# Making the low parts of split weights by accumulating transfers instead of VectorE subtractions

## The chip, the cores and the metric

One core of a Trainium2 chip. The metric is the device time of one execution in microseconds (us); lower is better.

## The reference, cut to what matters

Two layers over 1024 latent and 256 context tokens (NT = 1280 columns), everything in float32.

```python
xa, ga, ub, gb = split(h @ w_in)                     # layer 0, 3072 output channels
u = dwconv_centred(xa, conv_w, conv_b)               # 8 heads of 128 channels
r, i = sigmoid(u @ wr[d] + br), sigmoid(u @ wi[d] + bi)   # d = 0, 1: two directions
a = exp(-8 * r * softplus(-lam)); b = sqrt(-expm1(2 * log_a)) * (i * u)
ya = scan(a, b, forward) + scan(a, b, backward)      # RG-LRU recurrence
yb = s5(ub); yb = yb * sigmoid(gelu(yb) @ glu_w + glu_b)
out = concat([ya * silu(ga), yb * silu(gb)]) @ w_out # 12 blocks of 128 channels
# layer 1: latent attention, 8 heads; not touched by the change
```

## The kernel before, in words

A float32 product is computed as three matmuls of `fp32r` parts: each operand is split into a rounded high part `hi` and a low part `lo = x - hi`, and `mm3` adds hi·hi, hi·lo and lo·hi. The low part of a weight is needed first by the third matmul of a group, that of an activation by the second. Before the change every split is one ScalarE copy (`hi`, L182, L964, L1196) and one VectorE subtraction (`lo`, L184, L968, L1198).

Layer 0 runs in this order: a start; the recurrences of 8 heads; the output projection `out0`. The recurrences are written out by hand: `TURNS` is a list of words for turn 0 and 1, for turns 2 to 6 and for turn 7, and each engine executes its instructions in just that order. A word is a letter, arguments and an age (`-` is the head of the next turn). The words that matter here:

- `W`: splits a loaded weight tile (`wraw`, one buffer; `wh` and `wl`, two each) and then, in `load`, issues the next tile's load on SP's queue. `P`: one block of columns (256, 512 or 512) of the current tile's product; three make a tile. There are 18 tiles of gates and heads, 4 of `glu`, 16 of `out`; all but the first, which the start splits, go through `W`.
- `U`, `V`: load and split the gate weights of one direction of a head. `G`: a gate's product and its sigmoid.
- `C`: a tap of the convolution on VectorE. `I`, `O`: high and low part of a head's convolved input.
- `E`: one step of `s5_weights` (turns 0 and 1); its last step in each of 8 passes multiplies four groups of 32 output rows into one PSUM bank (L526, L529).
- `k a s r d o`: a batch of the S5 scan; `r` clears two columns by memsets on GpSimd (L1023, L1024), and VectorE's copy L1025 waits for them. `l` loads for it.
- `N`, `Y`: the scans of a head; its results go to DRAM by GpSimd's queue, the second one adding onto the first (`accum_op`, L953).
- In turn 7, `F` loads a head's result and gate, `S` multiplies them and splits the product (12 such pairs with `X` and `T` fill `self.mix` and `y`), `K` multiplies the S5 branch. Their tiles come from one pool of 11 slots (`big`); a load on SP's queue waits there until a slot is free, and all loads behind it wait too.

In `out0` the 16 `out` tiles run six `P` to a pair of tiles, with `W` after the first and the fourth.

Of the kernel before, what the change touches and what calls it, by code (L numbers as in the profile page):

```python
# [9 lines left out]
F32 = mybir.dt.float32  # L10
F32R = mybir.dt.float32r
AF = mybir.ActivationFunctionType
ALU = mybir.AluOpType
# [12 lines left out]
C1 = 6.28125  # L26
C2 = float(np.float32(np.round((2 * math.pi - C1) * 2 ** 21) / 2 ** 21))
# [5 lines left out]
def shape_constants():  # L33
# [18 lines left out]
    for a in (row, col):  # L52
# [13 lines left out]
     "E0 E0 E0 G000 E0 E0 E0 E0 V1- E0 E0 E0 V0- W0 A00 H00 P0 E0 E0 E0 E0 E0 E0 C0- P0 B00 "  # L66
     "W0 Y1 E0 A10 E0 Q00 E0 P0 E0 E0 E0 E0 E0 E0 C1- C2- I- P0 E0 O-").split(),
    ("D01 H11 M11 k21 U1- Q11 a21 G000 l00 N01 P0 G100 s21 B11 r21 U0- d21 D11 N11 W0 P0 o21 l10 a00 "
     "k00 s00 P0 r00 d00 C1- W0 Y1 P0 G110 o00 k10 G010 a10 C0- s10 M00 V0- V1- C2- A10 r10 A00 H00 I- Q00 "
     "d10 P0 O- l20 P0 B00 o10").split(),  # L70
# [62 lines left out]
class Kernel:  # L133
# [62 lines left out]

    def weight_parts(self, raw):
        return self.split(raw, self.wp, "w", 2, list(raw.shape))

    def raw_uk(self, h):  # L200
        return self.raw_weights(self.t["w_uk"][h], 2)
# [257 lines left out]
    def s5_weights(self, Pre, Pim, bb, ccp):  # L459

        nc, sp = self.nc, self.sp
        tt, stt = nc.vector.tensor_tensor, nc.vector.scalar_tensor_tensor
        scr = self.s5scr = self.dram.tile([16, 128, 4, 2, 128], F32, name="s5scr")

        seq = self.s5seq = self.dram.tile([32, 16, 256], F32, name="s5seq")
        vx = lambda *shape: self.tl(sp, [128, *shape], "vx", 4)
        b4 = lambda a, m: a.unsqueeze(2).to_broadcast([128, 4, m, 16])
        p4 = lambda a: a.unsqueeze(3).to_broadcast([128, 4, a.shape[2], 16])
        for Q in range(8):
            gs = slice(4 * Q, 4 * Q + 4)  # L470
            if Q % 4 == 0:

                Kt = self.tl(sp, [128, 4, 144], "s5K", 1)
                pads = []
                for k in range(2):
                    p = self.tl(sp, [128, 16, 32], "pad", 2)
                    nc.gpsimd.memset(p, 0.0)
                    hg = slice(4 * Q, 4 * Q + 16)
                    nc.vector.tensor_copy(p[0:64, :, 0:16], bb[0:64, k, hg])
                    nc.vector.tensor_copy(p[64:128, :, 16:32], bb[64:128, k, hg])  # L480
                    pads.append(p)

            Vs = []
            for k in range(2):
                V, x = vx(4, 8, 16), vx(4, 8, 16)
                pr, pi = p4(Pre[:, gs, 0:8]), p4(Pim[:, gs, 0:8])
                tt(x, pi, b4(bb[:, 1 - k, gs], 8), ALU.mult)
                tt(V, pr, b4(bb[:, k, gs], 8), ALU.mult)
                Vs.append((V, x))
                yield  # L490
            for k, (V, x) in enumerate(Vs):
                tt(V, V, x, ALU.subtract if k == 0 else ALU.add)
                pt = self.bank([128, 4, 128], "s5", 2)
                for g in range(4):
                    nc.tensor.transpose(pt[:, g], V[:, g].rearrange("p j h -> p (j h)"), self.ident)
                st = self.tl(sp, [128, 4, 128], "st", 2)
                nc.scalar.copy(st, pt)
                self.stores.append((scr[2 * Q:2 * Q + 2, :, k].rearrange("b p g n -> p b g n"),
                                    st.rearrange("p (b g) n -> p b g n", b=2)))
                yield  # L500

            Cs = []
            for k in range(2):
                C, x = vx(4, 9, 16), vx(4, 9, 16)
                pr, pi = p4(Pre[:, gs, 8:17]), p4(Pim[:, gs, 8:17])
                tt(x, pi, b4(ccp[:, 1 - k, gs], 9), ALU.mult)
                tt(C, pr, b4(ccp[:, k, gs], 9), ALU.mult)
                Cs.append((C, x))
                yield
            for k, (C, x) in enumerate(Cs):  # L510
                if k == 0:
                    tt(C, C, x, ALU.subtract)
                else:
                    stt(C, C, -1.0, x, ALU.mult, ALU.subtract)
                for b in range(2):
                    self.stores.append((scr[2 * Q + b, :, 2 + k],
                                        C[:, 2 * b:2 * b + 2, 1:9].rearrange("p g m h -> p g (m h)")))
                yield
            Cs = [C for C, _ in Cs]
            pk = self.bank([128, 144], "s5", 2)  # L520
            for g4 in range(4):
                g = 4 * Q + g4
                o = pk[32 * g4:32 * g4 + 32]
                for k in range(2):
                    C = Cs[k][:, g4].rearrange("p m h -> p (m h)")
                    nc.tensor.matmul(o[:, 16:144], pads[k][:, g % 16], C[:, 16:144], start=(k == 0), stop=(k == 1))  # L526
                for k in range(2):
                    both = bb[:, k, g:g + 2].rearrange("p g h -> p (g h)")
                    nc.tensor.matmul(o[:, 0:16], both, Cs[k][:, g4, 0], start=(k == 0), stop=(k == 1))  # L529
            nc.scalar.copy(Kt[:, Q % 4], pk)  # L530
            stt(Kt[:, Q % 4, 0:16], self.dmask, self.s5d[:, Q:Q + 1], Kt[:, Q % 4, 0:16], ALU.mult, ALU.add)
            if Q % 4 == 3:
                dst = seq[4 * Q - 12:4 * Q + 4].rearrange("(q g) h n -> g h q n", g=4)
                for g4 in range(4):
                    a = 32 * g4
                    self.stores.append((dst[g4, :, :, 128:256], Kt[a:a + 16, :, 0:128]))
                    self.stores.append((dst[g4, :, :, 0:128], Kt[a + 16:a + 32, :, 16:144]))
            yield
# [349 lines left out]
    def recurrences(self, steps):  # L888
# [3 lines left out]
        nc = self.nc  # L892
# [4 lines left out]
        class Head:  # L897
# [6 lines left out]
                nc.sync.dma_start(x.raw[d], self.t["gate_w"][x.h, :, 2 * d:2 * d + 2])  # L904

            def V(x, d):
                x.gw[d] = self.split(x.raw.pop(d), self.gp, "gw", 2, [128, 2, 128])

            def G(x, d, q):

# [53 lines left out]
                nc.scalar.copy(x.hi, self.us[x.h][0])  # L964

            def O(x):
                lo = self.big([128, NT], F32R, name="lo")
                nc.vector.tensor_sub(lo, self.us[x.h][0], x.hi.bitcast(F32))  # L968
                self.us[x.h] += x.hi, lo

        class Batch:
# [31 lines left out]
            def s(x):  # L1003

                x.t2 = self.s5t([128, 2, 2, NCH], "t2")
                x.G = self.s5t([128, 2, 2, EXT], "G")
                S = x.G[:, :, :, 0:NCH]
                for g in range(2):
                    tt(x.t2[:, :, g], x.ph[:, 1:3, g], x.p[g][:, ::-1], ALU.mult)
                    tt(S[:, :, g], x.p[g], x.ph[:, 0, g].unsqueeze(1).to_broadcast([128, 2, NCH]), ALU.mult)  # L1010
                tt(S, S, x.t2, ALU.add)
                nc.vector.tensor_copy(x.G[:, :, :, NCH:EXT], x.G[:, :, :, 0:32])
# [45 lines left out]
        class Tiles:  # L1058
            n, b, n_raw = 0, 0, 1
            raws, ws, ps = [], [self.first], {}  # L1060

            def load(x):
                if x.n_raw < len(tiles):
                    kind, i, _ = tiles[x.n_raw]
                    src, k = {"glu": (t["glu_w"], 4), "out": (t["w_out"], 6)}.get(kind, (t["w_in"], 8))
                    src = src[i // 2, :, 6 * (i % 2):6 * (i % 2) + 6] if kind == "out" else src[i]
                    x.raws.append(self.raw_weights(src, k))
                    x.n_raw += 1

            def W(x):  # L1070
                if x.raws:
                    x.ws.append(self.weight_parts(x.raws.pop(0)))
                    x.load()

            def P(x):
# [4 lines left out]
                kind, i, out = tiles[x.n]  # L1080
                b = x.b
                s, z = BLK[b]
                w = x.ws[0]
                src = {"glu": lambda: x.y, "out": lambda: self.mix[6 * (i % 2):6 * (i % 2) + 6]}.get(kind, lambda: self.n0)()
                if kind != "out" or i % 2 == 0:
                    x.ps[b] = self.bank([128, z], "g" if kind == "out" and i % 4 else "mm", 3)
                p, n = x.ps[b], len(src)
# [5 lines left out]
                elif kind == "gate":  # L1093
                    o = self.row((128, z))
# [11 lines left out]
                    x.ws.pop(0)  # L1106


            yg, y, g, gb, m, ga = {}, [None] * 4, {}, {}, {}, {}

            def Z(x, i):
                self.store()
# [19 lines left out]
                nc.sync.dma_start(x.ga[h], self.gadr[h])  # L1132

            def S(x, h):
                m, g = x.m.pop(h), x.ga.pop(h)
                nc.vector.tensor_mul(m, m, g)
                self.mix[h] = self.split_big(m, alloc=self.far)

            def J(x, i):
                x.gb[i] = self.big(name="gb")  # L1140
# [694 lines left out]
```

## Time and profile before

| | |
|---|---|
| time of three executions, median (lowest to highest) | 1578.91 us (1574.0 to 1582.47) |
| the profiled execution, its own time | 1579.79 us |
| its span, first to last instruction | 1577.7 us |
| mean granted TensorE clock | 0.981 |
| busy share of the span: TensorE, VectorE, ScalarE, GpSimd | 94%, 72%, 52%, 3% |

PE is TensorE's matmuls, PEld its weight loads, DVE is VectorE, ACT ScalarE, POOL GpSimd, SP the queue that issues most loads. L184 is line 184 of the kernel before. Clocks are shares of full speed. Busy shares are means over stages: turns 0 and 1 run from about 140 to 274 us, turns 2 to 6 to about 522, turn 7 to 655, `out0` to 820.

### The profile page before, as it was taken

The page shows a single profiled execution, that of the slowest core. Times are in us where ns is not written, and L with a number is a line of the kernel's source. Part 1 is how long each engine was busy: PE and PEld are TensorE (multiplying, and loading weights), DVE is VectorE, ACT ScalarE, POOL GpSimd, SP SyncE. Part 2 cuts the span into 40 slices and gives each one's busy share as a digit, 9 for nine tenths or more (in the row PEclk, how much of TensorE's full clock was granted, in tenths as well). Part 3 has the DMA queues.
Part 4 walks back from the last instruction along what each step waited for, and adds up shares of the span by engine and source line. Part 5 has one row for each costly group of instructions (what it writes and reads, how often), then busy time and mean ns, then how long its engine had stood idle before and what let it go on. Part 6 is the DMA issues. An engine that isn't in the chain of part 4 may idle for free.

```text
span 1577.7 us, 22599 instructions
## 1 busy us (share of the span) xinstructions
PE 1486.9 (94%) x8690; PEld 1277.5 (81%) x8690; DVE 1138.1 (72%) x1856; ACT 828.3 (52%) x1424; POOL 46.8 (3%) x107
## 2 busy tenths in 40 slices
PE   7899898988988996999999999999999999999997
PEld 4677777877777785878788999888999999999887
DVE  7678788999999888422255625558888888889655
ACT  7457766766866684110143414446555565566532
POOL 0001000000000000000000000010000000000000
PEclk9999999999999998999999999999999999999999
DMA  9355444644655555645351231451120120122353
GB/s 353 135 182 182 163 145 143 180 143 132 193 142 157 167 194 201 230 167 180 134 217 54 81 93 34 152 188 44 31 66 26 64 58 18 40 94 87 105 175 114
DMA packets 96154, 207.76 MB, mean 132 GB/s; under 512 B 9904, under 2 KB 42416, under 8 KB 96048
## 3 DMA queue, kind: packets, MB, share of 16 engines
q1 hardware_dynamic: 86528, 166.65, 32.3%
q0 software_dynamic: 9520, 39.69, 7.6%
q8 instruction: 68, 1.11, 0.3%
q14 instruction: 38, 0.31, 0.1%
HBM read 143.03 MB, written 63.28 MB: 131 GB/s over the span
## 4 chain that ended last, share of the span: by engine, by line
PE 35%; issue 26%; DVE 11%; DMA 2%; ACT 1%; POOL 1%; SPq 0%; DVEq 0%; POOLq 0%; ACTq 0%
PE pv L1580 7%; PE pt L1567 4%; PE S L209 2%; PE S L211 2%; PE S L210 2%; PE S L1519 2%; PE S L1518 2%; PE S L1517 2%; PE S L1516 2%; PE S L1515 2%; DVE H L1020 1%; PE mm L211 1%; PE mm L209 1%; PE mm L210 1%; PE pt L210 1%
## 5 line engine op out<-in xcount | busy, mean ns | idle before, releaser
L182 ACT CAST w_hi<-wraw 128x1024 fp32r<-128x1024 f32 (+3 forms) x73 | 63.3, 867 | 182.6 <-PE mm L210 130.5
L209 PE MATMUL mm<-n0hi,w_hi 128*128 128x512 f32 (+1 forms) x432 | 156.8, 363 | 0.0
L210 PE MATMUL mm<-n0lo,w_hi 128*128 128x512 f32 (+1 forms) x432 | 154.7, 358 | 0.0
L211 PE MATMUL mm<-n0hi,w_lo 128*128 128x512 f32 (+1 forms) x432 | 153.9, 356 | 0.0
L1571 ACT CAST ph<-pt 128x512 fp32r<-128x512 f32 x160 | 91.0, 590 | 83.2 <-PE pt L1567 82.9
L1574 DVE TENSOR_TENSOR pl<-pt,ph 128x512 fp32r<-128x512 f32 x160 | 109.5, 686 | 19.7 <-ACT ph L1571 17.7
L209 PE MATMUL mm<-hi,w_hi 128*128 128x512 f32 (+1 forms) x264 | 100.4, 380 | 11.5 <-ACT w_hi L182 9.5
L209 PE MATMUL mm<-n1hi,w_hi 128*128 128x342 f32 (+2 forms) x336 | 109.6, 329 | 1.7 <-DVE pr L1323 1.7
L210 PE MATMUL mm<-n1lo,w_hi 128*128 128x342 f32 (+2 forms) x336 | 110.2, 328 | 0.0
L211 PE MATMUL mm<-n1hi,w_lo 128*128 128x342 f32 (+2 forms) x336 | 110.1, 328 | 0.0
L1580 PE MATMUL pv<-ph,v 128*128 128x256 f32 x640 | 107.4, 298 | 0.0
L211 PE MATMUL mm<-hi,w_lo 128*128 128x512 f32 (+1 forms) x264 | 98.9, 378 | 5.1 <-DVE w_lo L184 5.1
L210 PE MATMUL mm<-lo,w_hi 128*128 128x512 f32 (+1 forms) x264 | 98.9, 375 | 0.1
L209 PEld LDWEIGHTS mm<-n0hi,w_hi 128*128 128x128 f32 x432 | 82.0, 190 | 12.8
L211 PEld LDWEIGHTS mm<-n0hi,w_lo 128*128 128x128 f32 x432 | 81.7, 189 | 12.7
L210 PEld LDWEIGHTS mm<-n0lo,w_hi 128*128 128x128 f32 x432 | 81.9, 190 | 12.1
L1567 PE MATMUL pt<-c_ident,P 128*128 128x128 f32 x640 | 90.9, 272 | 0.6 <-DVE kl L1497 0.6
L184 DVE TENSOR_TENSOR w_lo<-wraw,w_hi 128x1024 fp32r<-128x1024 f32 (+3 forms) x73 | 72.3, 991 | 25.9 <-ACT w_hi L182 24.9
L1552 ACT ACTIVATE P<-S,sm 128x512 f32<-128x512 f32 x128 | 86.8, 689 | 0.0
L1580 PEld LDWEIGHTS pv<-ph,v 128*128 128x128 f32 x640 | 84.3, 190 | 0.2
L1567 PEld LDWEIGHTS pt<-c_ident,P 128*128 128x128 f32 x640 | 75.7, 140 | 10.4 <-DVE kl L1497 0.8
L1544 DVE TENSOR_REDUCE sm<-S 128x1 f32<-128x512 f32 x128 | 82.0, 680 | 0.8 <-PE S L1519 0.8
(424 smaller groups left out, 4013.9 us busy)
## 6 DMA issues: line engine op xcount, KB each, us to landing
mw<-in_mod_w SPq DMA_DIRECT2D x48, 512.0 KB
wraw<-in_w_in SPq DMA_DIRECT2D x24, 512.0 KB
mixdr<-r POOLq DMA_DIRECT2D x14, 640.0 KB, 5.9
s5wt<-s5scr SPq DMA_DIRECT2D x16, 512.0 KB
ph<-phdr SPq DMA_DIRECT2D x16, 480.0 KB
wraw<-in_mla_in SPq DMA_DIRECT2D x14, 512.0 KB
wraw<-in_w_out SPq DMA_DIRECT2D x16, 384.0 KB
xT<-in_xT SPq DMA_DIRECT2D x8, 640.0 KB
```

The source lines that it names most:

```text
L182: nc.scalar.copy(hi, raw)
L184: nc.vector.tensor_sub(lo, raw, hi.bitcast(F32))
L209: mm(out, w[0], x[0], start=start, stop=False)
L210: mm(out, w[0], x[1], start=False, stop=False)
L211: mm(out, w[1], x[0], start=False, stop=stop)
L1515: mm(d, q[0][:, qs], k[0][:, ks], start=True, stop=False)
L1544: nc.vector.reduce_max(x.sm[e][:, n:n + 1], x.S[e][n], axis=mybir.AxisListType.X)
L1552: nc.scalar.activation(x.P[e][:, s:s + z], x.S[e][n], AF.Exp, bias=sm[:, 4:5], scale=SCALE, accum_out=sm[:, 5 + n:6 + n])
L1567: nc.tensor.transpose(pt[:, i, e], x.P[e][:, key:key + 128], self.ident)
L1571: nc.scalar.copy(x.hi[t], x.pt[t])
L1574: nc.vector.tensor_sub(x.lo[t], x.pt[t], x.hi[t].bitcast(F32))
L1580: mm(x.pv, v[:, 128 * (h % 2):128 * (h % 2) + 128], p, start=x.left == 30, stop=x.left == 1)
```

## The change

Weight tiles in `W`, gate weights in `V` and the convolved inputs in `O` get their low part so: ScalarE copies the high part, ScalarE writes its negative into the low tile, and a transfer issued by GpSimd adds the source (from DRAM for weights, from SBUF for `O`) onto it. `O` is moved ahead to stand right behind `I`. In `s5_weights` the loop over the two addends is moved outside the loop over the four row groups. In turn 7 each `S` now splits the product of the `S` before it (`due`); what is left is split by the first `P` that needs it.

```diff
-     ... A10 r10 A00 H00 I- Q00 d10 P0 O- l20 P0 B00 o10
+     ... A10 r10 A00 H00 I- O- Q00 d10 P0 l20 P0 B00 o10
+    def split_from(self, raw, src, pool, tag):
...
+        nc.scalar.copy(hi, raw)
+        nc.scalar.mul(lo, hi.bitcast(F32), -1.0)
+        nc.gpsimd.dma_start(lo, src.bitcast(F32R), accum_op=ALU.add)
+        return hi, lo
-            for g4 in range(4):
-                ...for k in range(2): matmul(o[:, 16:144], ...)
-                ...for k in range(2): matmul(o[:, 0:16], ...)
+            for k in range(2):
+                for g4 in range(4): matmul(pk[32*g4:32*g4+32, 16:144], ...)
+            for k in range(2):
+                for g4 in range(4): matmul(pk[32*g4:32*g4+32, 0:16], ...)
             def V(x, d):
-                x.gw[d] = self.split(x.raw.pop(d), self.gp, "gw", 2, [128, 2, 128])
+                x.gw[d] = self.split_from(x.raw.pop(d), self.t["gate_w"][x.h, :, 2 * d:2 * d + 2], self.gp, "gw")
             def O(x):
                 lo = self.big([128, NT], F32R, name="lo")
-                nc.vector.tensor_sub(lo, self.us[x.h][0], x.hi.bitcast(F32))
+                nc.scalar.mul(lo, x.hi.bitcast(F32), -1.0)
+                nc.gpsimd.dma_start(lo, self.us[x.h][0].bitcast(F32R), accum_op=ALU.add)
             def W(x):
-                    x.ws.append(self.weight_parts(x.raws.pop(0)))
+                    x.ws.append(self.split_from(*x.raws.pop(0), self.wp, "w"))
             def P(x):
+                if kind == "out" and None in self.mix[6 * (i % 2):6 * (i % 2) + 6]:
+                    x.parts()
             def S(x, h):
                 nc.vector.tensor_mul(m, m, g)
-                self.mix[h] = self.split_big(m, alloc=self.far)
+                x.parts()
+                x.due.append((h, m))
+            def parts(x):
+                while x.due:
+                    h, m = x.due.pop()
+                    self.mix[h] = self.split_big(m, alloc=self.far)
```

## Rows read from the trace of the kernel before

**Rows 1.** Busy time by stretch: us; PE, PEld, DVE, ACT, POOL busy; clock; DMA share; GB/s.
```profile
140.00:274.00 134.00, 118.39 (x755) 97.46 (x753) 114.98 (x158) 94.52 (x127) 9.65 (x13) 0.95 0.53 170
274.00:318.00 44.00, 41.29 (x213) 35.53 (x214) 40.43 (x45) 34.01 (x45) 1.80 (x6) 0.96 0.57 168
318.00:522.00 204.00, 179.78 (x965) 152.57 (x964) 198.21 (x225) 143.61 (x192) 8.03 (x32) 1.00 0.51 153
522.00:655.00 133.00, 114.07 (x557) 95.58 (x556) 106.19 (x87) 75.62 (x88) 1.81 (x6) 0.92 0.60 203
655.00:820.00 165.00, 165.00 (x902) 132.80 (x901) 46.29 (x75) 26.20 (x35) 3.74 (x7) 1.00 0.49 175
```
**Rows 2.** Waits of PE, 318 to 522 us: total, times, longest.
```profile
PE s L1040 <- DVE G L1033: 19.2, 12, 2.1
PE g L209 <- ACT r L917: 5.0, 4, 1.3
```
**Rows 3.** Groups of instructions by shape, 140 to 655 us: busy, mean ns, idle before.
```profile
L184 DVE TENSOR_TENSOR w_lo<-wraw,w_hi 128x1024 fp32r<-128x1024 f32 x17 | 20.6, 1214 | 5.4 <-ACT w_hi L182 5.4
L184 DVE TENSOR_TENSOR gw_lo<-gwraw,gw_hi 128x256 fp32r<-128x256 f32 x14 | 5.5, 419 | 1.0 <-ACT gw_hi L182 1.0
L968 DVE TENSOR_TENSOR lo<-u,hi 128x1280 fp32r<-128x1280 f32 x6 | 8.9, 1484 | 0.0
L182 ACT CAST w_hi<-wraw 128x1024 fp32r<-128x1024 f32 x17 | 18.0, 1056 | 0.0
L182 ACT CAST gw_hi<-gwraw 128x256 fp32r<-128x256 f32 x14 | 5.3, 422 | 0.0
```
**Rows 4.** The accumulating store L953 (640 KB): its issue in ns, its landing in us.
```profile
L953 POOL DMA_DIRECT2D mixdr<-r x7: 854/863/897, 236.7 to 545.9; - x7
...
DMA to landing us min/median/max: 5.8/6.2/6.7
```
**Rows 5.** The plain store L945 of the same size: its landing in us.
```profile
DMA to landing us min/median/max: 3.2/3.3/6.5
```
**Rows 6.** Timeline, end of turn 5: start, us, engine, line; ScalarE, GpSimd, VectorE, TensorE.
```profile
463.52 1.27 ACT L964 CAST hi<-u 128x1280 fp32r<-128x1280 f32 x1
...
466.99 0.10 POOL L1024 MEMSET H<- 64x4 f32 x1 [1.62 <-DVE H L1021]
...
469.72 1.49 DVE L968 TENSOR_TENSOR lo<-u,hi 128x1280 fp32r<-128x1280 f32 x1
...
472.77 0.28 PE L210 MATMUL g<-lo,gw_hi 128*128 128x256 f32 x1
```
**Rows 7.** Timeline of TensorE, one of eight passes of `E`: first and last matmuls.
```profile
213.07 0.62 PE L526 MATMUL s<-vx,pad 128*32 128x128 f32 x4
...
214.93 0.27 PE L529 MATMUL s<-vx,s5bb 128*32 128x16 f32 x4
```
**Rows 8.** Timeline of TensorE in turn 7: where it resumes after waiting.
```profile
545.57 0.39 PE L209 MATMUL g<-hi,gw_hi 128*128 128x256 f32 x1 [2.73 <-ACT r L917]
...
593.33 0.39 PE L209 MATMUL mm<-hi,w_hi 128*128 128x256 f32 x1 [0.83 <-ACT w_hi L182]
...
607.47 0.58 PE L211 MATMUL mm<-hi,w_lo 128*128 128x256 f32 x1 [0.45 <-DVE w_lo L184]
...
631.27 0.58 PE L211 MATMUL mm<-hi,w_lo 128*128 128x256 f32 x1 [3.84 <-DVE w_lo L184]
```
**Rows 9.** Waits of ScalarE, 522 to 655 us.
```profile
ACT hi L1196 <- DVE mixa L1136: 17.8, 6, 7.0
ACT row L1095 <- DMA gadr<-row: 9.0, 2, 7.0
```
**Rows 10.** Timeline of SP's queue in turn 7: the load of the last `glu` tile.
```profile
607.44 0.33 SPq L194 DMA_DIRECT2D wraw<-in_glu_w  x1
```
**Rows 11.** Timeline in `out0`: a weight tile's copy, and its first matmul.
```profile
667.58 0.83 ACT L182 CAST w_hi<-wraw 128x768 fp32r<-128x768 f32 x1 [10.45 <-PE g L210]
...
678.09 0.28 PE L209 MATMUL mm<-hi,w_hi 128*128 128x256 f32 x1
```

More of the change, by code (lines that the diff above doesn't have):

```diff
@@ L68 @@
     ("D01 H11 M11 k21 U1- Q11 a21 G000 l00 N01 P0 G100 s21 B11 r21 U0- d21 D11 N11 W0 P0 o21 l10 a00 "
-     "k00 s00 P0 r00 d00 C1- W0 Y1 P0 G110 o00 k10 G010 a10 C0- s10 M00 V0- V1- C2- A10 r10 A00 H00 I- Q00 "
-     "d10 P0 O- l20 P0 B00 o10").split(),
+     "k00 s00 P0 r00 d00 C1- W0 Y1 P0 G110 o00 k10 G010 a10 C0- s10 M00 V0- V1- C2- A10 r10 A00 H00 I- O- Q00 "
+     "d10 P0 l20 P0 B00 o10").split(),
     ("Z20 M11 G110 a21 k21 H11 D01 s21 B11 N01 r21 l00 Q11 W0 P0 P0 Z10 d21 P0 G100 D11 N11 o21 G000 W0 "
@@ L198, in weight_parts @@
         return self.split(raw, self.wp, "w", 2, list(raw.shape))
+    def split_from(self, raw, src, pool, tag):
+        nc = self.nc
+        self.n += 1
+        hi, lo = (pool.tile(list(raw.shape), F32R, name=f"{tag}_{n}_{self.n}", tag=tag + n[0], bufs=2) for n in ("hi", "lo"))
+        nc.scalar.copy(hi, raw)
+        nc.scalar.mul(lo, hi.bitcast(F32), -1.0)
+        nc.gpsimd.dma_start(lo, src.bitcast(F32R), accum_op=ALU.add)
+        return hi, lo
     def raw_uk(self, h):
@@ L520, in s5_weights @@
             pk = self.bank([128, 144], "s5", 2)
-            for g4 in range(4):
-                g = 4 * Q + g4
-                o = pk[32 * g4:32 * g4 + 32]
-                for k in range(2):
+            for k in range(2):
+                for g4 in range(4):
                     C = Cs[k][:, g4].rearrange("p m h -> p (m h)")
-                    nc.tensor.matmul(o[:, 16:144], pads[k][:, g % 16], C[:, 16:144], start=(k == 0), stop=(k == 1))
-                for k in range(2):
+                    nc.tensor.matmul(pk[32 * g4:32 * g4 + 32, 16:144], pads[k][:, (4 * Q + g4) % 16], C[:, 16:144],
+                                     start=(k == 0), stop=(k == 1))
+            for k in range(2):
+                for g4 in range(4):
+                    g = 4 * Q + g4
                     both = bb[:, k, g:g + 2].rearrange("p g h -> p (g h)")
-                    nc.tensor.matmul(o[:, 0:16], both, Cs[k][:, g4, 0], start=(k == 0), stop=(k == 1))
+                    nc.tensor.matmul(pk[32 * g4:32 * g4 + 32, 0:16], both, Cs[k][:, g4, 0], start=(k == 0), stop=(k == 1))
             nc.scalar.copy(Kt[:, Q % 4], pk)
@@ L1066, in load @@
                     src = src[i // 2, :, 6 * (i % 2):6 * (i % 2) + 6] if kind == "out" else src[i]
-                    x.raws.append(self.raw_weights(src, k))
+                    x.raws.append((self.raw_weights(src, k), src))
                     x.n_raw += 1
@@ L1106, in P @@
                     x.ws.pop(0)
-            yg, y, g, gb, m, ga = {}, [None] * 4, {}, {}, {}, {}
+            yg, y, g, gb, m, ga, due = {}, [None] * 4, {}, {}, {}, {}, []
             def Z(x, i):
```

## The prediction

> **What bounds the kernel now.** I read the page first: TensorE is busy for 94% of the span, so only stages in which it idles can give time back. The table by stretch shows them [rows 1]. In `out0` (655 to 820 us) PE is busy 165.00 of 165.00 us: nothing to win there, only to lose. Turns 3 to 6 (318 to 522) are four equal stretches of 51.0 us: VectorE is busy 198.21 / 4 = 49.55 us of each, TensorE 179.78 / 4 = 44.95, ScalarE 143.61 / 4 = 35.9. These turns are VectorE's. The list of PE's waits names it: 19.2 us in 12 waits of the S5 output product for VectorE, and 5.0 us for ScalarE's sigmoids [rows 2], 4.8 and 1.25 us a turn. Turn 2 (274 to 318) has PE idle for 2.7 us, turns 0 and 1 for 134.00 - 118.39 = 15.6 us with VectorE idle for 19.0: there neither engine paces alone. In turn 7 (522 to 655) PE idles for 18.9 us, mostly for weights split shortly before use [rows 8], and ScalarE stands 17.8 us at high parts waiting for products of `S` [rows 9].
>
> **Part 1: weights, gate weights and `O` in turns 3 to 6.** A turn has two `W`, two `V` and one `O`. VectorE loses 2 x 1.214 + 2 x 0.419 + 1.484 = 4.75 us [rows 3], from 49.55 to 44.8. ScalarE's negative reads and writes what its copy does, so I price it as the copy: 2 x 1.056 + 2 x 0.422 [rows 3] + 1.27 [rows 6] = 4.2 us, from 35.9 to 40.1; no trace of this kernel shows the operation, and anything from nothing to twice the copy leaves ScalarE under 45. TensorE is then next, with 44.95 us of work and the 1.25 us of waits for sigmoids, 46.2 in all; its waits for the S5 branch should go as VectorE runs ahead.
>
> The transfers are new. The nearest row is the accumulating store of 640 KB from SBUF to DRAM: 0.86 us on GpSimd to issue, 5.8 to 6.7 us to land, median 6.2 [rows 4]; plain, the same size lands in 3.3 [rows 5]. Here the destination is SBUF, and no row shows that; bounds are 3.2 and 6.7 us, and I take 6.2 for `O` (640 KB) and 5 for the weights (128 to 512 KB).
>
> The weights of these turns are split long before use: a tile made by either `W` is first read two or more `P` later, some 11 us at 5.6 us a `P` (24 matmuls of 0.234), or after a turn's other work. Copy, negative, issue and landing are 1.06 + 1.06 + 0.9 + 5 = 8 us: hidden, but with only 3 us to spare in the tightest case. `wraw` is free after the copy, not after the subtraction, so SP's next loads go out sooner.
>
> `O` is not so well hidden. At the end of turn 5 the copy starts at 463.52, and the second matmul of the next head's gate needs `lo` at 472.77; before, VectorE had it at 471.21 [rows 6]. Now: copy to 464.8, negative to 466.1, but GpSimd's queue holds the second memset of `r` ahead of the issue, at 466.99; the issue is at 467.1 and 6.2 us later it is 473.3, 0.5 us late. Two gate weights' negatives (0.84 us) stand ahead of the copy on ScalarE too. Bounds: no stall (landing 3.2), or 2.5 (6.7 and the issue on top of it). I take 1.5 us of PE stall a turn. What queues behind the waiting instructions is harmless: behind `O`'s issue on GpSimd come the head's store and the next batch's memsets, some 11 us later; behind `V`'s are the memsets of the third `r`, 4.5 us later.
>
> So a turn goes from 51.0 to 44.95 + 1.25 + 1.5 = 47.7: 3.3 us, **13.2 us** in four. Bounds: 0 if stalls eat it, 4 x 4.75 = 19.0 if VectorE's whole relief counts. For turn 2 I take **1.7** of PE's 2.7 us idle (bounds 0 and 2.7).
>
> **Part 2: turns 0 and 1.** VectorE loses 4 x 1.214 + 4 x 0.419 + 1.484 = 8.0 us, ScalarE gains 4 x 1.056 + 4 x 0.422 + 1.27 = 7.2. With neither engine pacing alone I count a third, 2.7 us. The reordered loops issue the same matmuls; a pass took from 213.07 to 215.20, 2.1 us for 32 records [rows 7], 17 us in eight passes. Four neighbours in a row now go to different output rows rather than adding onto what the one before wrote. I take 0.1 us a pass, 0.8 in all. Sum **3.5** (bounds 0 and 15.6, all of PE's idle time).
>
> A rule speaks for more: the Trainium skill, "TensorEngine Tiling (Array Packing)", section "Tiling Modes", says that tiles of the array operate independently, so that different ones load weights and multiply in parallel. By it a pass could shrink by up to four, to 0.5 us, and the sum would be 12 us lower. The row speaks against most of that: four records already start within 0.62 us of each other's end, 65 ns a record on average, before any reordering.
>
> **Part 3: turn 7.** Its first half gains. SP's queue stood at the reload of `wraw` until VectorE's subtraction, and stores of gate rows behind it kept ScalarE from its row buffers (7.0 us, the longest wait of that kind) [rows 9], which held PE for 2.73 us [rows 8]. The reload now waits for the copy alone: I take off 2.7 us.
>
> The second half has short leads: a `glu` tile's first use is one `P` after its `W`. A tile takes PE 7.0 us (blocks of 1.4, 2.8 and 2.8: 36 matmuls, 0.117 or 0.234 each). In the times of before: PE was done with the first tile at 592.5 (593.33 less 0.83 of waiting) [rows 8], so its second block ended at 589.7. Behind that block's sigmoid (0.7) the second tile's copy can start at 590.4, since no `S` stands in front of it on ScalarE any more; copy 0.6 and negative 0.6 (between the rows for 256 and 1024 columns [rows 3]), landing 5: 596.6, a new wait of 4.1 us. The third tile's copy follows the sigmoid of the next block at 596.6 + 1.4 + 0.5 = 598.5: ready at 604.7, PE gets there at 603.6 and waits 1.1; it resumes 2.8 sooner than before, at 607.47 [rows 8]. The fourth tile's load left SP's queue at 607.44 [rows 10], behind loads that wait for free slots; each `S` now keeps its product until the next one, one tile more in 11 slots, so I let it go at 608. It lands by 614, then 0.6 + 0.6 + 5: 620.2, where PE wants it at 611.7. The first `out` tile follows 7.0 us later, at 627.2; behind a high part of `T` (1.27) its copy and negative (0.83 each) and 5 us end at 635.1, with before 631.27 [rows 8]: 3.8 later. Some of the later blocks run at the lower clock (0.92 in the mean of this stage [rows 1]), so I say 5. With 2.7 from the first half turn 7 is 2.3 us longer, **2.5** (bounds: 6 shorter with landings of 3.2 us and a free slot, 10 longer with 6.7). The deferred splits take 17.8 us of waits off ScalarE [rows 9], but PE waits for weights there, and only the one copy above becomes earlier.
>
> A second rule bears on this: the Trainium skill, "DMA: Bandwidth & Descriptors", section "Anatomy of one DMA", prices a transfer of GpSimd's at about 2.0 us and its bytes at 436 GB/s, an estimate of 2.6 us for 256 KB. By it turn 7 would be shorter by some 5 us and no `O` late. The rows disagree: by the rule 640 KB take 3.5 us, near the plain row (3.3), not the accumulating one (6.2).
>
> **Part 4: `out0`.** 13 subtractions leave VectorE, which is idle for most of the stage; no gain. A tile's copy starts at 667.58 and its first matmul at 678.09: 10.5 us of lead [rows 11]. Needed: 0.83 + 0.83 + 0.9 + 5 = 7.6. Cost nothing; if the landing takes over 7.9 us, each further microsecond is paid 13 times.
>
> **Sum.** 1579.8 (profiled execution's own time) - 13.2 - 1.7 - 3.5 + 2.5 = 1563.9. The median of the runs shown, 1578.9, is 0.9 lower; I forecast **1564**.
>
> **Rivals.**
> - *The wait moves.* PE waits for `O`'s transfer, ScalarE's and GpSimd's queues couple VectorE to PE, and a turn gains 1 us instead of 3.3; turn 7 costs 5. Then 1579.8 - 4 - 1 - 3 + 5 = 1577. For it: 0.5 us late by the rows already, all engines over 80% busy. Against it: PE's 4.8 us of waits a turn are for VectorE alone. Chance 0.17.
> - *Slow accumulation in `out0` (slower).* With other loads running (DMA share 0.49) and an SBUF destination a landing takes 11 us: 3.1 over the lead, 13 times, is 40 us, and turn 7's four late tiles cost 20 more: 1579.8 + 40 + 20 - 5 = 1635. It decides from about 9.2 us on, where 13 x 1.3 cancels the gains. For it: nothing but the unknown form. Against it: at most 6.7 us in seven records. A landing of 9.5 to 10 would give 1590 to 1600. Chance 0.10.
> - *The reordered passes run in parallel.* 12 us of PE's time in turns 0 and 1 go: 1552. Chance 0.11. By the tiling rule above.
> - *Forecast*, 1556 to 1572: 0.62.
>
> **Numbers.** About 0.5%, 8 us, can be told from no change here: faster is under 1571, slower over 1587. Faster: nearly all of 0.62 and 0.11, less a twentieth: 0.71. Same: the first rival and that edge, 0.20. Slower: 0.09. The range for 8 in 10 runs from 1549 (the third rival's side) to 1580 (the first rival's).
>
> **What would show each step.** VectorE's busy time falls by 4.75 us a turn, ScalarE's grows by 4.2, the turns' period falls from 50.9 to under 48.5, and PE's waits for the S5 branch fall below 2 us a turn. A new wait of the gate's second matmul for a transfer, 0 to 2.5 us. The transfers land in 3 to 7 us. PE waits longer behind weight splits of turn 7. `out0` stays at 165 us. The passes of `E` stay near 2 us. The forecast is wrong if transfers land in over 8 us, if ScalarE becomes the bound of a turn, or if PE's waits change owner instead of going.

## The result, and the profile after

The changed kernel takes 1589.77 us (median of 8 runs, 1584.79 to 1598.51) against 1579.19 for the kernel before beside it (8 runs): ratio 1.0081, 95% interval 1.0056 to 1.0105. The forecast was 1564, in a range from 1549 to 1580; the kernel became slower. The profiled execution has a span of 1588.9 us at a mean clock of 0.972 (before 1577.7 and 0.981).

In the kernel after, `split_from` is L199 to L208 (copy L205, negative L206, transfer L207), `O`'s copy, negative and transfer are L976, L981 and L982, the forward scan in `N` is L955, the `E` matmuls are L535 and L541, `mm3`'s three are L219 to L221, and the first store of `out0` is L1253. Busy time by stretch in the kernel after, columns as in [rows 1]:

```profile
140.00:274.00 134.00, 110.74 (x719) 90.74 (x720) 107.54 (x149) 98.73 (x132) 18.13 (x24) 0.90 0.66 188
274.00:318.00 44.00, 34.07 (x206) 29.11 (x205) 27.58 (x32) 29.00 (x43) 4.79 (x8) 0.88 0.74 193
318.00:522.00 204.00, 189.82 (x1008) 160.73 (x1007) 190.84 (x215) 169.26 (x221) 27.38 (x57) 1.00 0.77 200
522.00:655.00 133.00, 104.63 (x514) 88.00 (x514) 95.31 (x74) 85.62 (x100) 8.94 (x15) 0.90 0.74 223
655.00:820.00 165.00, 163.60 (x891) 131.47 (x890) 32.14 (x54) 34.52 (x42) 15.44 (x21) 1.00 0.68 199
```

The steady turns (third row) are what was meant: TensorE is busier than before, 189.82 against 179.78 us. Turn 2 and turn 7 (second and fourth rows) are worse: TensorE loses 7.2 and 9.4 us of busy time against [rows 1], and the granted clock goes from 0.96 to 0.88 in turn 2. The list of TensorE's waits from 130 to 850 us says for what:

```profile
PE mm L221 <- DMA w_lo<-in_glu_w: 11.7, 3, 7.5
PE g L220 <- DMA lo<-u: 10.0, 2, 8.0
PE mm L221 <- DMA w_lo<-in_w_out: 8.7, 1, 8.7
...
PE mm L221 <- DMA w_lo<-in_w_in: 5.5, 2, 3.0
...
PE mm L219 <- ACT w_hi L205: 2.8, 2, 2.7
```

Four of these groups are waits for the new transfers, 35.9 us in eight waits. Before, the waits for the same parts were 5.1 us for the low parts of late weights and 2.0 us for head 2's `O`. The kernel before also waited longer for the high parts of the same tiles:

```profile
PE mm L209 <- ACT w_hi L182: 8.9, 3, 4.8
...
PE mm L211 <- DVE w_lo L184: 5.1, 4, 3.8
```

Both kinds together were 14.0 us for the `glu` and `out` tiles of turn 7; they are now 2.8 + 11.7 + 8.7 = 23.2. What left is the wait for VectorE's S5 branch, 19.2 us in [rows 2]. From 318 to 522 us the list of the kernel after is:

```profile
PE s L1015 <- ACT y L1057: 5.7, 4, 1.4
PE g L219 <- ACT r L929: 5.0, 4, 1.3
PE g L219 <- ACT i L929: 2.1, 4, 0.5
PE s L1054 <- DVE G L1047: 1.3, 5, 0.3
```

To see where the time went I follow the eight forward scans (L943 before, L955 after) and the first and last store of `out0`. Single executions reach the start of turn 0 up to 4.5 us apart in code that the change doesn't touch, so the first column counts from a row ahead of it, the first phase of the S5 weights on VectorE (124.5 us before, 124.7 after). Stretches in us, each the difference of two starts in the timeline, rounded to 0.1 us first, so the last digit can be off by one:

| kernel | to 1st scan | 1st to 2nd | 2nd to 3rd | 3rd to 6th | 6th to 8th | 8th to first store | `out0` |
|---|---|---|---|---|---|---|---|
| before | 99.0 | 54.9 | 44.7 | 152.4 | 94.9 | 85.0 | 164.6 |
| after | 100.7 | 54.7 | 51.5 | 145.3 | 93.3 | 94.3 | 166.2 |
| difference | +1.7 | -0.2 | +6.8 | -7.1 | -1.6 | +9.3 | +1.6 |

The differences sum to 10.5 us, the 10.6 of the medians. The middle of the table gained, from 50.8 to 48.4 us a turn; the entry to turn 2 and the second half of turn 7 lost 16 us.

**Entry to turn 2.** The kernel after, ScalarE, GpSimd and TensorE:

```profile
275.16 1.26 ACT L976 CAST hi<-u 128x1280 fp32r<-128x1280 f32 x1 [3.18 <-DVE u L884]
...
276.97 1.28 ACT L981 ACTIVATE lo<-hi 128x1280 fp32r<-128x1280 f32 x1
...
278.55 0.84 POOL L982 DMA_DIRECT2D lo<-u  x1 [12.86 <-ACT lo L981]
...
276.47 0.39 PE L219 MATMUL g<-hi,gw_hi 128*128 128x256 f32 x1 [1.29 <-ACT hi L976]
284.85 0.58 PE L220 MATMUL g<-lo,gw_hi 128*128 128x256 f32 x1 [7.99 <-DMA lo<-u]
...
285.87 0.63 PE L220 MATMUL g<-lo,gw_hi 128*128 128x512 f32 x1
```

This is head 2's `O`. TensorE has its first gate matmul done and then stands for 7.99 us, until the transfer issued at 278.55 lands 6.3 us later. With VectorE's subtraction the same wait was 1.95 us, in the kernel before:

```profile
275.76 0.39 PE L210 MATMUL g<-lo,gw_hi 128*128 128x256 f32 x1 [1.95 <-DVE lo L968]
```

Behind the stall of 7.99 us the engine is at its lower level: the granted clock is 0.50 from 285 to 288 us, and a matmul over 512 columns takes 0.63 us, against 0.39 in a row of turn 7 below.

The other of the two waits for an `O` stands at the entry to turn 7:

```profile
516.74 1.25 ACT L976 CAST hi<-u 128x1280 fp32r<-128x1280 f32 x1
...
524.76 0.58 PE L220 MATMUL g<-lo,gw_hi 128*128 128x256 f32 x1 [1.99 <-DMA lo<-u]
```

So from the copy's start to the read TensorE left `O` 276.86 - 275.16 = 1.7 us at the entry to turn 2 and 522.77 - 516.74 = 6.0 us at the entry to turn 7, where it needed 9.7 and 8.0. In the turns between it is 8.7 us (468.31 to 476.99, for one), and no wait is listed.

**Turn 7.** The second `glu` tile (first four rows) and the first `out` tile:

```profile
590.93 0.62 ACT L205 CAST w_hi<-wraw 128x512 fp32r<-128x512 f32 x1
591.58 0.63 ACT L206 ACTIVATE w_lo<-w_hi 128x512 fp32r<-128x512 f32 x1
...
592.51 0.84 POOL L207 DMA_DIRECT2D w_lo<-in_glu_w  x1 [21.82 <-ACT w_lo L206]
...
591.05 0.39 PE L221 MATMUL mm<-hi,w_lo 128*128 128x512 f32 x1
...
599.58 0.58 PE L221 MATMUL mm<-hi,w_lo 128*128 128x256 f32 x1 [7.48 <-DMA w_lo<-in_glu_w]
...
630.42 0.83 ACT L205 CAST w_hi<-wraw 128x768 fp32r<-128x768 f32 x1
...
632.42 0.84 POOL L207 DMA_DIRECT2D w_lo<-in_w_out  x1 [15.64 <-ACT w_lo L206]
...
640.80 0.58 PE L221 MATMUL mm<-hi,w_lo 128*128 128x256 f32 x1 [8.70 <-DMA w_lo<-in_w_out]
```

From GpSimd's issue to TensorE's restart are 7.1 us for 256 KB and 8.4 us for 384 KB; the two `glu` tiles between them take 8.1 and 5.7. The issues of transfers in the kernel after, with size and median landing in us over the whole kernel, against 6.2 in [rows 4]:

```profile
w_lo<-in_w_in POOLq DMA_DIRECT2D x17, 512.0 KB, 6.0
...
w_lo<-in_w_out POOLq DMA_DIRECT2D x16, 384.0 KB, 7.1
...
lo<-u POOLq DMA_DIRECT2D x6, 640.0 KB, 5.4
...
gw_lo<-in_gate_w POOLq DMA_DIRECT2D x16, 128.0 KB, 6.0
...
w_lo<-in_glu_w POOLq DMA_DIRECT2D x4, 256.0 KB, 6.3
```

The landing hardly depends on the size: 128 KB take as long as 512 KB from DRAM, and the 640 KB of `O`, from SBUF, are the quickest.

**A pass of `E`**, the pair of rows that answers to [rows 7]:

```profile
216.35 0.64 PE L535 MATMUL s<-vx,pad 128*32 128x128 f32 x16
216.81 0.29 PE L541 MATMUL s<-vx,s5bb 128*32 128x16 f32 x16
217.03 0.39 PE L219 MATMUL g<-hi,gw_hi 128*128 128x256 f32 x1
```

The pass's 16 matmuls (32 records) hold TensorE for 0.7 us instead of 2.1; passes with a wait or a lower clock in them take up to 1.2 us instead of up to 2.6. Before, the first four records, all for one block of output rows, start at 213.07 and what follows starts at 213.53, 0.46 us later. Now sixteen records for four blocks take the same 0.46 us (216.35 to 216.81).

### The profile page after: what moved, and what is told of

The parts are those of the page before. It is cut to its first block, busy times and chain, and to the rows that moved or that the text cites. A ratio compares the mean times of both kernels' runs of the same rounds, so it can differ in the third digit from the quotient of the medians.

```text
span 1588.9 us, 22734 instructions
## 1 busy us (share of the span) xinstructions
PE 1481.5 (93%) x8690; PEld 1273.6 (80%) x8690; DVE 1090.0 (69%) x1797; ACT 874.1 (55%) x1483; POOL 97.3 (6%) x166
## 4 chain that ended last, share of the span: by engine, by line
PE 52%; issue 21%; ACT 6%; DMA 4%; DVE 4%; POOL 1%; SPq 0%; POOLq 0%; DVEq 0%; ACTq 0%
PE pv L1603 7%; PE mm L219 5%; PE mm L221 5%; PE mm L220 5%; PE pt L1590 4%; PE S L219 2%; PE S L221 2%; PE S L220 2%; PE S L1542 2%; PE S L1541 2%; PE S L1540 2%; PE S L1539 2%; PE S L1538 2%; PE g L219 1%; DMA w_lo<-in_w_out 1%
## 5 line engine op out<-in xcount | busy, mean ns | idle before, releaser
L221 PE MATMUL mm<-n0hi,w_lo 128*128 128x512 f32 (+1 forms) x432 | 156.1, 361 | 5.5 <-DMA w_lo<-in_w_in 5.5
L219 PE MATMUL mm<-n0hi,w_hi 128*128 128x512 f32 (+1 forms) x432 | 158.6, 367 | 0.0
L1594 ACT CAST ph<-pt 128x512 fp32r<-128x512 f32 x160 | 90.9, 589 | 83.1 <-PE pt L1590 82.7
L221 PE MATMUL mm<-hi,w_lo 128*128 128x512 f32 (+1 forms) x264 | 99.1, 378 | 20.4 <-DMA w_lo<-in_glu_w 11.7
L219 PE MATMUL mm<-n1hi,w_hi 128*128 128x342 f32 (+2 forms) x336 | 109.6, 329 | 1.6 <-DVE pr L1346 1.6
L221 PE MATMUL mm<-n1hi,w_lo 128*128 128x342 f32 (+2 forms) x336 | 110.6, 329 | 0.0
L219 PE MATMUL mm<-hi,w_hi 128*128 128x512 f32 (+1 forms) x264 | 100.1, 379 | 7.0 <-ACT w_hi L205 2.8
L221 PEld LDWEIGHTS mm<-n0hi,w_lo 128*128 128x128 f32 x432 | 83.6, 194 | 18.7 <-DMA w_lo<-in_w_in 5.9
L219 PEld LDWEIGHTS mm<-n0hi,w_hi 128*128 128x128 f32 x432 | 83.7, 194 | 12.7
L182 ACT CAST w_hi<-wraw 128x1024 fp32r<-128x1024 f32 (+3 forms) x36 | 29.6, 822 | 111.4 <-PE mm L220 99.3
L1590 PEld LDWEIGHTS pt<-c_ident,P 128*128 128x128 f32 x640 | 75.7, 141 | 10.4 <-DVE kl L1520 0.8
L221 PEld LDWEIGHTS mm<-hi,w_lo 128*128 128x128 f32 x264 | 51.5, 195 | 31.1 <-DMA w_lo<-in_glu_w 12.4
```

Of the source, the lines that this page charges most:

```text
L219: mm(out, w[0], x[0], start=start, stop=False)
L221: mm(out, w[1], x[0], start=False, stop=stop)
L1590: nc.tensor.transpose(pt[:, i, e], x.P[e][:, key:key + 128], self.ident)
L1594: nc.scalar.copy(x.hi[t], x.pt[t])
```

## The experiments

Times are medians of 4 to 12 runs, and ratios are against the kernel before beside them, which had medians of 1577.51 (27 runs, the first four), 1578.09 (23, the next four) and 1578.12 (11, the last four). Stretches of the profiled executions, in the columns of the table above:

| kernel | us | to 1st | 1-2 | 2-3 | 3-6 | 6-8 | 8-store | `out0` |
|---|---|---|---|---|---|---|---|---|
| e1 | 1587.5 | 101.5 | 54.1 | 44.5 | 145.2 | 93.4 | 97.5 | 166.4 |
| e2 | 1576.2 | 101.2 | 52.6 | 51.0 | 145.2 | 92.3 | 83.1 | 164.6 |
| e3 | 1572.1 | 101.6 | 59.2 | 43.5 | 145.2 | 92.3 | 83.2 | 164.6 |
| e4 | 1573.4 | 94.5 | 53.6 | 44.5 | 152.4 | 94.8 | 85.8 | 164.6 |
| e5 | 1560.5 | 94.5 | 52.6 | 43.7 | 145.2 | 92.7 | 82.8 | 164.6 |
| e6 | 1575.8 | 95.0 | 52.4 | 48.8 | 145.4 | 89.8 | 92.6 | 164.7 |
| e7 | 1576.7 | 99.0 | 54.9 | 44.7 | 152.5 | 94.9 | 83.9 | 164.6 |
| e8 | 1561.4 | 94.4 | 52.5 | 43.7 | 145.2 | 92.8 | 86.3 | 164.5 |
| e9 | 1568.8 | 99.1 | 54.0 | 43.7 | 145.3 | 93.8 | 82.4 | 164.6 |
| e10 | 1561.5 | 94.1 | 52.8 | 44.4 | 145.3 | 93.9 | 83.3 | 164.6 |
| e11 | 1560.8 | 94.4 | 52.5 | 46.3 | 147.9 | 91.0 | 83.3 | 164.0 |
| e12 | 1569.9 | 98.8 | 54.7 | 43.7 | 145.3 | 94.4 | 82.8 | 164.6 |

**e1: head 2's `O` by VectorE.**

```diff
+                if x.h == 2:
+                    nc.vector.tensor_sub(lo, self.us[x.h][0], x.hi.bitcast(F32))
+                else:
                     nc.scalar.mul(lo, x.hi.bitcast(F32), -1.0)
                     nc.gpsimd.dma_start(lo, self.us[x.h][0].bitcast(F32R), accum_op=ALU.add)
```

> The changed kernel, but the low part of head 2's input (the only one split by turn 1's list, where O stands at the very end) is made by VectorE's subtraction. Theory (the loss is transfers that land after their first use): TensorE's 8.0 us wait for that transfer at the start of turn 2 goes, and 2 us of subtraction wait come back as before: 6 us and a little clock less than the changed kernel, about 1583. Rival (the added transfers and ScalarE work slow the stages evenly): one transfer of 59 makes under 1 us, about 1589. Second rival (TensorE only waits elsewhere, for ScalarE, which is behind anyway): 1587.

1587.5, ratio 1.0067 (1.0041 to 1.0092), 2.3 less than after. The stretch from the 2nd to the 3rd scan gets its 7.0 us back, 51.5 to 44.5, so the cause of that loss is shown. The time is not the 1583 of the theory but what I gave for the second rival, TensorE waiting elsewhere (1587), and a difference of 2.3 us is within the overlap of the two intervals. In the execution shown turn 7's second half is 3.2 us longer than after, with 2.1 us more of waits for late tiles; why they grew is open.

```profile
PE mm L221 <- DMA w_lo<-in_glu_w: 13.9, 3, 5.8
PE mm L221 <- DMA w_lo<-in_w_out: 8.6, 1, 8.6
```

**e2: the `glu` and `out` tiles by VectorE.**

```diff
+                    vec = 18 <= x.n_raw - 1 < 99   # tiles 18 to 21 are glu, 22 to 37 out
-                    x.ws.append(self.split_from(*x.raws.pop(0), self.wp, "w"))
+                    x.ws.append(self.weight_parts(raw) if vec else self.split_from(raw, src, self.wp, "w"))
```

> The changed kernel, but the 4 glu and 16 out weight tiles (turn 7 and out0) are split by VectorE's subtraction as before. Theory (late transfers): TensorE's waits of 11.7 us for glu and 8.7 us for out tiles go, some 8 us of waits for the copy and the subtraction come back: 9 to 12 us less than the changed kernel, about 1579. Rival (the held product of S, one tile more in the pool of 11 slots, is what costs turn 7): the time stays within 3 us of 1590, since S is unchanged here.

1576.2, ratio 0.9993 (0.9981 to 1.0006): 13.6 us below after, 11 of them in turn 7's second half (94.3 to 83.1) and 1.6 in `out0`. TensorE's waits for these tiles from 560 to 660 us fall from 11.7 + 8.7 to:

```profile
PE mm L221 <- DVE w_lo L184: 6.4, 2, 4.5
```

**e3: both.** The edits of e1 and e2 together.

> Both edits together. Theory (two places of late transfers, independent): the two savings add, 15 to 18 us less than the changed kernel, about 1573, faster than the kernel before by some 6 us, which is what turns 3 to 6 gain. Rival (waits only move): the savings do not add, 1580 or more.

1572.1, ratio 0.9963 (0.9947 to 0.9979). As expected, the savings of e1 and e2 add (2.3 and 13.6, 17.6 together): with the late tiles out of the way, head 2's `O` is worth 4.1 us. In this execution a wait for a weight tile of turn 1 (one of two, 9.1 us in all) lengthens the stretch from the 1st to the 2nd scan to 59.2:

```profile
PE mm L221 <- DMA w_lo<-in_w_in: 9.1, 2, 4.7
```

**e4: the kernel before with the loops over the passes reordered, and nothing else.**

```diff
+            for k in range(2):
+                for g4 in range(4): matmul(pk[32*g4:32*g4+32, 16:144], ...)
+            for k in range(2):
+                for g4 in range(4): matmul(pk[32*g4:32*g4+32, 0:16], ...)
```

> The kernel before with nothing but the reordered loops of the eight passes in turns 0 and 1. Theory (a pass's matmuls were not bound by the accumulation order): a pass stays near 2 us, the time within 3 us of before, 1579. Rival (the reordered passes are what makes turns 0 and 1 longer, through more idle time of TensorE and a lower clock there): 3 to 5 us slower, 1583. Rival of the other sign (row groups run in parallel): a pass of 0.5 to 1 us, up to 10 us faster.

1573.4, ratio 0.9968 (0.9956 to 0.998): 4.1 us gained by an edit that I had at 0.8; the rival that a pass falls under 1 us holds, and my theory of no change falls. The first scan comes 4.5 us earlier and the second a further 1.3. It also turns the accounts around: measured from this kernel, all the transfers of e3 together bring 1.3 us, though they shorten three turns by 7.2. What they lose, they lose ahead of the second scan: 101.6 against 94.5 to the first, and 59.2 against 53.6 from there.

**e5: transfers only where they have time**, in turns 2 to 6.

```diff
+                    vec = not 5 <= x.n_raw - 1 <= 17       # W: tiles of turns 0 and 1, glu and out by VectorE
+                if x.h <= 2:                           # V of heads up to 2
+                    x.gw[d] = self.split(x.raw.pop(d), self.gp, "gw", 2, [128, 2, 128])
+                if x.h <= 2:                           # O of heads up to 2
+                    nc.vector.tensor_sub(lo, self.us[x.h][0], x.hi.bitcast(F32))
```

> The change kept where its transfers have time (the two heads' weights, gate weights and convolved inputs of turns 2 to 6), VectorE's subtraction where they are read soon after (turns 0 and 1; tiles 18 to 37, the glu and out tiles); reordered passes and later splits of S kept. Theory (the transfers cost in turns 0 and 1 what they win later, because there and in turn 7 a tile is read about one P after it is split): turns 0 and 1 as with the reordered loops alone (first forward scan near 217.4, second near 271), turns of 48.4 us in place of 50.8, the end as without late transfers: 1573.4 - 3 x 2.4 - 1 = 1565, between 1562 and 1568. Rival (turns 0 and 1 lose by the slower clock that reordered passes bring with them, not by the transfers): first scan near 224, 1572. Rival (turn 7 waits for something that does not move with the turns): 1571 to 1573, with steady turns of 48.4 all the same.

1560.5, ratio 0.989 (0.9872 to 0.9909), the fastest of all (e8, e10 and e11 are within 1.0): 29.3 us below after, 17.6 below before, and 1.5 below the range that I gave. The first scan stands where e4 has it, the turns run at 48.4 us, and turn 7 keeps what they win. Both rivals fall. Turns 3 to 6 by stretch, columns as in [rows 1]:

```profile
318.00:522.00 204.00, 189.13 (x1010) 160.38 (x1009) 188.47 (x215) 167.71 (x222) 26.01 (x55) 1.00 0.76 205
```

**e6: plain transfers in place of adding ones.** The low parts then hold the raw values.

```diff
-        nc.gpsimd.dma_start(lo, src.bitcast(F32R), accum_op=ALU.add)
+        nc.gpsimd.dma_start(lo, src.bitcast(F32R))
```

> The kernel after, with every transfer onto a negative part made a plain transfer; the low parts then hold the raw values, so part of the computation is changed, the instructions and bytes are the same. Theory A (adding is what makes the transfers slow): they land in 3 to 4 us as the plain ones of the same size do, the waits of turn 7 (7.5, 3.7 and 8.7 us) fall to 3, 0 and 4, head 2's wait of 8.0 us to 5, and the time to 1576. Theory B (the queue is slow by contention with the loads that go out at the same moments, whatever the transfer does): landings stay at 6 to 8 us and the time at 1588.

1575.8, ratio 0.9983 (0.9968 to 0.9999): 14 us below after. Medians of landings in e6:

```profile
w_lo<-in_w_in POOLq DMA_DIRECT2D x17, 512.0 KB, 5.3
...
w_lo<-in_w_out POOLq DMA_DIRECT2D x16, 384.0 KB, 5.0
...
lo<-u POOLq DMA_DIRECT2D x6, 640.0 KB, 3.3
...
gw_lo<-in_gate_w POOLq DMA_DIRECT2D x16, 128.0 KB, 5.6
...
w_lo<-in_glu_w POOLq DMA_DIRECT2D x4, 256.0 KB, 4.3
```

Adding costs 2.0 to 2.1 us for `O`, the `glu` and the `out` tiles, and 0.4 to 0.7 for the others; GpSimd is also held for 0.53 us by an issue instead of 0.84. The time is theory A's, the landings only for `O`: the weights still take 4.3 to 5.6 us. In turn 7 8.2 us of waits for two `glu` tiles and 6.5 for an `out` tile are left. From the 6th scan to the first store the kernel after takes 187.6 us, e6 182.4 and e2, which splits these tiles on VectorE, 175.4. So of the 12.2 us that transfers cost there, adding is 5.2, and making the tile through any transfer so shortly before its use is the other 7.0; ahead of the first scan (95.0 against 100.7, and 94.5 in e4) adding is nearly all. These stretches are of one execution, of 1569.2 us, the shortest of e6. Whether the loads that go out at the same moments slow the plain ones was not tried alone; the DMA engines were busy for all of 592 to 599.5 us, the stall for the second `glu` tile in the kernel after.

**e7: the kernel before with the later splits of `S`'s products.**

```diff
-                self.mix[h] = self.split_big(m, alloc=self.far)
+                x.parts()
+                x.due.append((h, m))
```

> The kernel before with only the later splits of S's products. The prediction's step: takes 17.8 us of waits off ScalarE but PE waits for weights there, so 1577.5, within 1.5. Rival (those waits held up the weight copies): forward half of turn 7 and its second half 2 to 4 us shorter, 1574.

1576.7, ratio 0.9993 (0.9983 to 1.0003): nothing that can be told, as expected.

**e8: e5 with `S` split at once.**

> The first kernel of this call with S split at once as before the change. If the later splits matter neither way: the same as the first kernel within 1.5 us. Rival (with transfers the ScalarE queue needs them out of the way): 3 us longer than the first kernel, with PE's waits in 560 to 640 us longer by as much.

1561.4, ratio 0.9893 (0.9877 to 0.991), 0.9 above e5 in 4 and 6 runs. The profiled executions differ by 3.5 us in turn 7's second half, the medians don't bear that out. The deferral is no part of the result.

**e9: e5 with the weight tiles of turns 0 and 1 by transfer again.**

```diff
-                    vec = not 5 <= x.n_raw - 1 <= 17
+                    vec = not 1 <= x.n_raw - 1 <= 17
```

> The mixed kernel with the four weight tiles of turns 0 and 1 by transfer again. Theory (turns 0 and 1 lose by weight tiles that are read one P after their split: waits of 4.5 and 4.7 us for w_lo in the traces, and a lower clock behind them): most of the 6.5 us that the first forward scan comes later with transfers is back; 1560.5 + 6 = 1566.5, waits of PE for w_lo of 5 to 9 us. Rival (it is the gate weights and head 1's convolved input): 1561.5, within 1.

1568.8 (1560.8 to 1571.5), ratio 0.9934 (0.9913 to 0.9955): 8.3 above e5, more than the 6 expected. The first scan is 4.6 us later and the second a further 1.4. TensorE's waits from 140 to 285 us:

```profile
PE mm L221 <- DMA w_lo<-in_w_in: 3.6, 2, 1.8
PE s L535 <- DVE vx L522: 3.2, 2, 2.2
```

3.6 us are for the tiles themselves, less than I expected, and the wait of the `E` pass for VectorE, 1.0 us in e5, is longer. That these four tiles carry most of the loss of turns 0 and 1 is shown, 6.0 us to the second scan of the 7.3 by which the kernel after is behind e4; how its parts follow from one another is not.

**e10: e5 with the other transfers of turns 0 and 1.** `V` of all heads and `O` of head 1.

```diff
-                if x.h <= 2:      # O by VectorE
+                if x.h == 2:
```

> The mixed kernel with the gate weights of turns 0 and 1 and head 1's convolved input by transfer again (head 2's stays with VectorE). Theory: these are read long after their split; 1561.5, within 1. Rival: 1566.5.

1561.5, ratio 0.9893 (0.9879 to 0.9908): 1.0 above e5, within the noise. As expected, these cost nothing that can be told.

**e11: e5 with every `O` by VectorE.**

```diff
-                    nc.scalar.mul(lo, x.hi.bitcast(F32), -1.0)
-                    nc.gpsimd.dma_start(lo, self.us[x.h][0].bitcast(F32R), accum_op=ALU.add)
+                nc.vector.tensor_sub(lo, self.us[x.h][0], x.hi.bitcast(F32))
```

> The mixed kernel with every O by VectorE's subtraction; weights and gate weights of turns 2 to 6 still by transfer. VectorE gets 1.48 us of work a turn back, 45.3 + 1.5 = 46.8 of a period of 48.4. The prediction's step (O's transfer stalls PE by 1.5 us a turn and this is what holds the period above 46.2): the period falls to 47, the time to 1556. Rival (O's transfer costs nothing in these turns; the period is PE's 45 and its 3.4 us of waits for ScalarE): period 48.4 to 49, 1560 to 1563.

1560.8, ratio 0.9886 (0.987 to 0.9903), as e5. The period is 49.3 us, 0.9 longer, and the wait that comes back, from 318 to 522 us, is the one for the S5 branch:

```profile
PE s L1056 <- DVE G L1049: 10.8, 12, 1.7
```

So `O`'s transfer does not set the steady period, as the rival had it (1560 to 1563); it is worth 0.9 us a turn there. Between the 6th and the 8th scan e11 is 1.7 us shorter than e5, which waits 2.4 us for `O` at the entry to turn 7. The whole kernel shows neither: e11's profiled execution reaches the first store 3.9 us later than e5's, its median is 0.4 higher.

**e12: e5 with the old order of the passes.**

> The mixed kernel with the loops over the passes of E in the order of before. Alone, the new order is worth 4.1 us (1577.5 to 1573.4). If the parts add up: 1560.5 + 4.1 = 1564.6, first forward scan 4.5 us later. Rival (with later stages shorter the start of turn 2 is set by VectorE, and the new order wins nothing): 1561.

1569.9 (1561.8 to 1572.1), ratio 0.9938 (0.9917 to 0.9959): 9.4 above e5, the first scan 4.3 us later and the second a further 2.1. So the parts don't add up to 1564.6, and the rival (1561) falls too: the order matters at least as much in the mixed kernel as alone. How much more is not sure, with runs 10 us apart.

## Why the prediction was wrong

**Turns 3 to 6 (13.2 us): the mechanism held, the size did not.** VectorE's 4.75 us a turn went: at 48.4 us a turn, the 204 us of its stretch hold 4.21 turns, so it is busy for 45.3 us of each (44.8 predicted), TensorE for 45.0 (44.95) and ScalarE for 40.2 (40.1). The price of the negative was right: 1061 ns beside 1055 for its copy. The period is 0.7 us over the 47.7 forecast. The `O` stall of 1.5 us a turn that I had put there is not in the list of this stretch; it came once, with 1.99 us, at the entry to turn 7. In its place TensorE waits 1.43 us a turn for ScalarE's copy of the S5 branch's output (5.7 in four) and 0.5 for a second sigmoid (2.1 in four): with VectorE out of the way, ScalarE's order of work came last. Three turns gave 7.1 us. The fourth interval ends in turn 7: from the 6th to the 7th scan it is 56.0 us against 55.1 before, where the sum had it 3.3 shorter, with that stall in it. From the 7th to the 8th the kernel is 2.4 us shorter, near the 2.7 that I had for turn 7's first half.

**Turn 2 (1.7 us gained; 6.8 lost): the step that failed most plainly.** I worked `O` out once, at the end of turn 5, and used that for every turn. The list of words for turns 0 and 1 ends in `O-`, with the gate of head 2 as its reader right at the start of the next list; the read was due 1.7 us after the start of the copy, where turns 3 to 6 leave 8.7. The landing there was 6.3 us, about the 6.2 that I had taken. It was the cover that I had not looked for, and the stall that I had put at nothing. e1 and e3 show it.

**Turns 0 and 1 (3.5 us gained; 1.5 lost).** Two terms were wrong and opposed. The reorder is worth 5.8 us to the second scan in e4, not 0.8. I argued from four records within 0.62 us that they already ran together; but in the same 0.46 us from first record to next block, sixteen run in the new order. It was the rival that I gave 0.11, in direction: the pass went from 2.1 to 0.7 us, and eight of them free 11 us of TensorE, of which 4.1 reach the end alone and, by the medians, 9.4 beside the transfers of e5. That is the rule of the Trainium skill, "TensorEngine Tiling (Array Packing)", section "Tiling Modes": tiles work independently; the trace agrees, with 2.1 to 0.7 us, once neighbours go to different output rows. Against it stood the weight tiles: "I count a third" covered a term for which I had not looked at the distance from `W` to the first use. In this list it is short: in turn 0 a tile's copy starts at 189.76 and TensorE needs its low part at 195.04, 5.3 us later, and has it 3.04 us late, at 198.08. e9 shows what such tiles cost.

**Turn 7's second half (5.2 us lost; 9.3).** The places were right: all four late tiles that I named stall TensorE or come late. The size was off by the landing, 5 us in the sum, and 7.1, 8.1, 5.7 and 8.4 in the trace, and by what follows from one late tile to the next: the third tile's copy waits for a block behind the second's stall, at the lower clock (0.50 from 599.6 to 603 us), and starts at 602.49, where I had 598.5. I had dates of 596.6, 604.7, 620.2 and 635.1; TensorE resumed at 599.58, 612.18, 621.61 and 640.80. I had taken the weights below the only adding row that there was, 6.2 us in [rows 4], because they are smaller, and no row said that size matters. The Trainium skill, "DMA: Bandwidth & Descriptors", section "Anatomy of one DMA", has about 2.0 us and the bytes at 436 GB/s, an estimate of 3.5 us for 640 KB and 2.9 for 384. e6 agrees with it for a plain `O` (3.3 us) and not for plain `out` tiles (5.0); the adding ones, 5.4 and 7.1, are far from it.

**`out0` (0; 1.6 lost).** The lead of 10.5 us held: 0.83 + 0.84 + about 0.3 until the issue + 7.1 is 9.1, and all tiles but one come in time; that one is waited for 1.4 us. (A landing counts from the start of the issue, so the 0.9 us for the issue in the forecast's sums, here and for the weights of turns 3 to 6, was counted twice; it decided nothing.) The rival of slow accumulation had its place here and is wrong for it; its other half, the late tiles of turn 7, happened. The deferred splits were costed at nothing, and e7 shows that.

**The rivals.** "The wait moves" is nearest: waits for transfers took the place of waits for VectorE. But I let it take back the gains of steady turns, where there was room. It struck where the list of work differs from the steady one.

## What to carry to other kernels

A split through a transfer is worth it where a subtraction's engine paces the stage and the part is read late: here e5, with transfers in turns 2 to 6 alone, beats both kernels, 1560.5 us against 1578.1 and 1589.8. Before pricing such a change from the steady loop, list every place where it is used and measure, in each, the time from the source's arrival to the first read: here it had to cover 8 to 10 us (from the copy's start to the restart: 8.0 and 9.7 for `O`, 8.7 and 10.4 for weights in the rows shown), and the three places with less cost 22: the start of turn 0 (100.7 against 94.5 with the reorder alone), the entry to turn 2 (6.8) and turn 7 (9.3). An edit that comes along with another, like the reorder, should be timed alone, since its gain hides the other's loss.

## What the runs showed of the hardware

- An adding transfer into SBUF lands in 5.4 to 7.1 us by medians, up to 10.3 for an `out` tile, and as late for 128 KB as for 512 KB (6.0 each, from DRAM). The same transfers without adding take 3.3 to 5.6, and hold GpSimd for 0.53 us instead of 0.84.
- A pass of 16 small matmuls (32 records) onto four blocks of 32 output rows takes 0.7 us when neighbours in time go to different blocks, and 2.1 us when each block is finished before the next.
- Behind the stall of 7.99 us the granted clock was 0.50, the lower of its two levels (1.2 GHz): 0.63 us for a matmul over 512 columns against 0.39. In the kernel before it was 0.63 us too, at 276.62, behind the stall of 1.95 us. The mean clock of turn 2 went from 0.96 to 0.88, and from 628 to 648 us, in turn 7, it is 0.66 where it was 0.83. At the entry to turn 2 the wait grew by 6.0 us and the stretch by 6.8.
